# One branch to a whole copy of an expert, in place of a branch in each of its steps

## The chip, the cores and the metric

The kernel runs on one core of a Trainium2 chip. Times are device microseconds of one execution; less is better. The kernel before takes 1640.35 us, the median of 3 runs.

## The reference

The program is a two-layer encoder on 512 tokens of 1024 features. Layer 0 has a neighbourhood attention and a dense SwiGLU; layer 1 has a latent attention and a mixture of eight experts, of which each token takes two. The change touches the experts alone. There the reference runs every expert on all tokens and weighs the results; the weight is zero where a token has not chosen the expert:

```python
probs = softmax(hf @ w_router)
vals, idx = lax.top_k(probs, 2)
wts = vals / jnp.sum(vals, axis=-1, keepdims=True)
combine = jnp.sum(one_hot(idx, 8) * wts[..., None], axis=1)
y = 0
for e in range(8):
    gate, up = split(hf @ w_gu[e], 2)          # 1024 x 3584
    y = y + combine[:, e:e+1] * ((silu(gate) * up) @ w_down[e])   # 1792 x 1024
```

## The kernel before

The experts are called e0 to e7 here, as the code counts them; the words of the change, "two to seven", are e1 to e6. The kernel gathers for each expert only the rows that chose it. How many these are is known when the program runs, not before. The first 128 rows are the first block, done for every expert; rows 129 to 256 are the second block. A second block of at most 64 rows is done in the form "few" (its rows packed beside each other, `few_rows`, 8 or 16 matmuls where the whole form has 24), a larger one in the form "many", and an expert with 128 rows or fewer has none. In the traced execution e1 is few, e2 and e7 are many, and e0, e3, e4, e5 and e6 have no second block, as the lines show that run in them.

An expert has 11 steps. Steps 0 to 6 multiply the rows by gate and up weights (24 matmuls of 128 x 512 a block), make `act`, and transpose it in the next step into `A` (`turn`, `store_turn`). Steps 7 to 10 multiply `A` by the down weights. Each weight arrives by DMA (queued by SP), is cast to a rounded high part `hi` by ACT, and VectorE subtracts to get the low part `lo`; three matmuls (hi x hi, hi x lo, lo x hi) make one product in nearly full precision. `emit_to` issues the loads and casts of a later step beside the matmuls of this one.

The order is written out by hand: on each engine the instructions stand in the order of the code, and the loop over `steps` is unrolled. What depends on the number of rows stands in branches. `second_block(n, many, few)` is a branch on the register `n` (L1483) and within it one between many and few (L1487), on every engine. Two of them stand in every step. One runs the matmuls of the second block. The other, `flush()`, runs what the step before owed to the second block (the list `pend`): its `act`, its transposes' copies, or its output. The copy that is taken of a branch and the one that isn't must leave the semaphores with the same counts; in a path that skips work, an engine therefore waits until its own earlier work is done and then adds the skipped ticks, in one semaphore instruction. `count(e)` (L1479) loads the number of rows of an expert to a register of each engine; it stands in step 1 of the expert ahead (step 3 for e0). The rows of the next expert are gathered there and transposed in steps 7 and 8 (`rows0`), those of its second block in step 9 (`second_rows`).

Of the kernel before, what the change touches and what calls it, by code (L numbers as in the profile page):

```python
# [9 lines left out]
F32 = mybir.dt.float32  # L10
# [46 lines left out]

class Kernel:
    def __init__(self, ctx, tc, d, dbg=None):
        self.ctx, self.tc, self.nc, self.d = ctx, tc, tc.nc, d  # L60
        self.dbg = dbg
        pool = lambda name, bufs, **kw: ctx.enter_context(tc.tile_pool(name=name, bufs=bufs, **kw))
        self.consts = pool("consts", 1)
        self.big = pool("big", 3)
        self.rawp = pool("raw", N_RAW)
        self.splitp = pool("split", N_SPLIT)
        self.dram = pool("dram", 1, space=DRAM)
        self.Y = self.dram.tile([(NE - 1) * CAP, D], F32, name="Y")
        self.jobs = []
        self.done = {}  # L70
        self.emitted = 0
        self.loaded = {}
        self.ada_acc = None
        self.ada_rows = []
        self.extra = None
        self.raw_slots, self.raw_no = [], -1
        self.piece = self.pool_every = 0

    def add_slots(self, pool, n, big, raw_pool, n_raw):
# [3 lines left out]
        self.slots = ["split"] * N_SPLIT + ["extra"] * n + ["big"] * big  # L83
        self.raw_slots = [raw_pool] * n_raw + [0, 1] + [self.rawp] * N_RAW
# [46 lines left out]
    def raw_tile(self, shape):  # L131
# [5 lines left out]
        t = self.big_raw[:, pool] if pool in (0, 1) else pool.tile([P, 2048], F32, name="raw", tag="raw")  # L137
# [5 lines left out]
    def split_tiles(self, shape, pool=None):  # L143
        n = int(np.prod(shape[1:]))
        kind = "split"
        if pool is None and self.extra is not None:
            self.turn_no += 1
            kind = self.slots[self.turn_no % len(self.slots)]
        if kind == "big":
            both = [self.big_split[:, i, 0:n] for i in range(2)]  # L150
        else:
            pool = pool or (self.extra if kind == "extra" else self.splitp)
            both = [pool.tile([P, 2048], F32R, name=w, tag=w)[:, 0:n] for w in ("hi", "lo")]
# [935 lines left out]
    def router(self, small, hp, ps_a, ps_b, ps_c, cst):  # L1089
# [64 lines left out]
        def rest(R, C, T, idx0, ps_y):  # L1154
# [41 lines left out]
            ps = ps_y.tile([P, S], F32, name="y", tag="y")  # L1196
# [12 lines left out]
            ps = ps_y.tile([P, S], F32, name="y", tag="y")  # L1209
# [19 lines left out]
    def moe_phase(self, xT, oH, oL):  # L1229
        nc, tc, d = self.nc, self.tc, self.d  # L1230
        with ExitStack() as es:
# [64 lines left out]
            self.add_slots(split, N_EXTRA, N_BIG, turns.enter_context(tc.tile_pool(name="moe_raw", bufs=N_RAWX)), N_RAWX)  # L1296
            A = st.tile([P, 14, 512], F32R, name="a")
# [9 lines left out]

            def rows_tile():
                return w1.tile([P, D], F32, name="xb")
# [15 lines left out]
            def rows0(he, t, h, b=0, ps=None):  # L1325
                if ps is None:
                    ps = ps_t.tile([P, S], F32, name="tp", tag="tp")
# [42 lines left out]
            def out_rows(e, n, b, ps):  # L1370
                yo = w2.tile([P, S], F32, name="yo")
# [3 lines left out]

            def act_tile():
                return w2.tile([P, 256], F32, name="act0")
# [23 lines left out]
            def few_out(e, n, ps):  # L1401
                gs = w2.tile([P, S], F32, name="yo")[0:FEW]
# [5 lines left out]
            def overflow():  # L1408

                iota, tokid = cst[:, 0:128], cst[:, 128:132]  # L1410
                with tc.tile_pool(name="over", bufs=1, side="right") as op:
# [4 lines left out]
                    ps = ps_t.tile([P, S], F32, name="tp", tag="tp")  # L1416
# [10 lines left out]
                    with tc.For_i(0, NE, 1) as e:  # L1427
# [10 lines left out]
                        for j in range(7):  # L1438
                            pss = [ps_gu.tile([P, S], F32, name="gu", tag="gu") for _ in range(2)]
# [6 lines left out]
                            for b in range(2):  # L1446
                                a = act_tile()
                                swiglu(a, pss[b])
                                ps = ps_t.tile([P, S], F32, name="tp", tag="tp")
                                turn(a, ps)  # L1450
                                store_turn(A, j, b, ps)
                        for n in range(2):
                            pss = [ps_y.tile([P, S], F32, name="y", tag="y") for _ in range(2)]
# [6 lines left out]
                            for b in range(2):  # L1460
                                t = w2.tile([P, S], F32, name="yo")
                                nc.vector.tensor_scalar_mul(t, pss[b], cur[:, 1, 0, b:b + 1])
                                yo.append(t)
                            for i in range(4):
                                ps = ps_gu.tile([P, S], F32, name="gu", tag="gu")
# [8 lines left out]
                for i in range(4):  # L1474
                    for n in range(3):
                        self.square_sum(x_tok, w2, ssq, n, i)
# [3 lines left out]

            def second_block(n, many, few):

                with tc.If(n > P):  # L1483
# [34 lines left out]
            tail = rest(scratch[:, 0:1024], scratch[:, 1024:1280], w2.tile([P, S], F32, name="yo"), idx0, ps_y)  # L1518
            next(tail)
            for i in range(4):  # L1520
                for h in range(2):
                    ps = ps_gu.tile([P, S], F32, name="gu", tag="gu")
# [8 lines left out]
            rows0(he_next, xb0, 1, ps=ps_y.tile([P, S], F32, name="y", tag="y"))  # L1531
# [10 lines left out]
            def weigh(cols, ps, b=0):  # L1542

                for b, p in enumerate(ps, b):
                    t = w2.tile([P, S], F32, name="yo")[:, cols]
# [4 lines left out]
            for i, (e, s) in enumerate(steps):  # L1550
                emit_to(2 * i + PRE)
                n, g = divmod(s - 7, 2)
                ws = [self.done[k][0:2] for k in step_jobs(i)]
                if s == 0:
                    n_reg, he = n_next, he_next
                    act0 = None
                if s == (3 if e == 0 else 1) and e < last:
                    n_next = count(e + 1)
                    xb0 = rows_tile()
                    gather(xb0, HT, idx, 4 * (e + 1))  # L1560
                    with tc.If(n_next > P):
                        gather(xb1, HT, idx, 4 * (e + 1) + 1)
                owe = lambda *f: pend.append(f)
                if s < 7 or g == 0:
                    second.reverse()
                    ps1 = second[0]
                parts = [ALL] if e < last or s < 9 else HALVES if s == 9 else HALVES[0:1]
                if s < 7:
                    ps = ps_gu.tile([P, S], F32, name="gu", tag="gu")
                    for t in range(2):  # L1570
                        gate_up(ps, he, 0, t, ws[t])
                    flush()
                    pend_reg, pend_few = n_reg, e < last
                    prev, act0 = act0, act_tile()
                    swiglu(act0, ps)
                else:
                    if g == 0:
                        pys = [ps_y.tile([P, S], F32, name="y", tag="y") for _ in parts]
                        py = pys[0]
                    for b, cols in enumerate(parts):  # L1580
                        for t in range(2):
                            down(pys[b], A, 0, 2 * g + t, ws[t], cols)
                    flush()
                    prev = act0 if s == 7 else None
                if prev is not None:
                    ps = ps_t.tile([P, S], F32, name="tp", tag="tp")
                    turn(prev, ps)
                    store_turn(A, s - 1, 0, ps)
                    owe(lambda A=A, j=s - 1: store_turn(A, j, 1, tp1), lambda A=A, j=s - 1: few_store(A, j))
                if s < 7:  # L1590
                    owe(lambda ps=ps1: swiglu(act1, ps), lambda ps=ps1: few_swiglu(ps))

                def many():
                    for t in range(2):
                        if s < 7:
                            gate_up(ps1, he, 1, t, ws[t])
                    if s >= 7:
                        for ps, cols in zip(second, parts):
                            for t in range(2):
                                down(ps, A, 1, 2 * g + t, ws[t], cols)  # L1600
                    if prev is not None:
                        turn(act1, tp1)

                def few():
                    for t in range(2):
                        if s < 7:
                            few_rows(ps1, he, ws[t], 4 * t, 4 * t + 4, KD)
                        else:
                            k0 = 8 * g + 4 * t
                            few_rows(ps1, A, ws[t], k0, min(14, k0 + 4), 14)  # L1610
                    if prev is not None:
                        few_turn()

                if i == 0:
                    second_rows(n_reg, he, True, second[1])
                second_block(n_reg, many, few if e < last else None)
                if s >= 7 and g == 1 and e < last:
                    out_rows(e, n, 0, py)
                    owe(lambda e=e, n=n, ps=ps1: out_rows(e, n, 1, ps), lambda e=e, n=n, ps=ps1: few_out(e, n, ps))
                if e == last:  # L1620
                    if s == 0:
                        turns.close()
                        late = pool("moe_late", 1)
                        self.raw_slots = [self.rawp]
                        gf_row = late.tile([P, D], F32, name="gf_row")
                        fn_row = late.tile([P, D], F32, name="fn_row")
                        x_tok = self.big_raw.rearrange("p a (b c) -> p (a b) c", b=2)
                        nc.scalar.dma_start(gf_row, self.GF.broadcast_to([P, D]))
                        nc.scalar.dma_start(fn_row, d["final_norm"].rearrange("(o n) -> o n", o=1).broadcast_to([P, D]))
                        for t in range(4):  # L1630
# [199 lines left out]
```

## Time and profile before

| | |
|---|---|
| median of 3 runs | 1640.35 us (1640.19 to 1643.37) |
| profiled execution: its time | 1640.96 us |
| its span | 1639.2 us |
| PE (TensorE) busy | 1568.3 us, 96% |
| VectorE busy | 1109.6 us, 68% |
| ACT (ScalarE) busy | 817.1 us, 50% |
| experts e0 to e7, start to end | 927.9 to 1639.2 us of the span |
| e3, e4, e5, e6: from first matmul to that of the next expert | 65.9, 66.2, 66.0, 67.2 us |

An expert without a second block has 14 x 2 + 8 small transposes and 252 large matmuls, one each 0.23 us. PE's matmul instructions are taken up by a sequencer that runs ahead of the array; branches, register loads and semaphore instructions run on that sequencer (PEq and PEldq in the rows), and they are not counted as busy. An idle time in brackets is put down to what came last by the trace before the instruction started.

### The profile page before, as it was taken

Reading aid. Unit: us, or ns where it says so; the run is one execution under the profiler, and the core shown is the slowest. Engines: PE = TensorE matmul, PEld = TensorE weight load, DVE = VectorE, ACT = ScalarE, POOL = GpSimd, SP = SyncE. Lnnn points to the kernel's source line nnn. Section 1 sums busy time; section 2 is a strip of 40 time slices with the busy share of each in tenths; the row PEclk is TensorE's granted clock in tenths of the full one; section 3 lists DMA queues with packets and bytes.
Section 4 is the critical chain, followed back from the end, with each engine's and each line's share of the span. In section 5 each row is a group of like instructions: output and inputs, shape, how many; then the busy total and the mean of one; then the engine's idle time right before and its main releaser. Section 6 shows DMA issues by size and latency. Waiting matters only on the chain. (4 is left out here: it accounts for less than half of the span.)

```text
span 1639.2 us, 23888 instructions
## 1 busy us (share of the span) xinstructions
PE 1568.3 (96%) x8293; PEld 1266.4 (77%) x8293; DVE 1109.6 (68%) x1701; ACT 817.1 (50%) x1382; POOL 295.3 (18%) x250
## 2 busy tenths in 40 slices
PE   6899999999999999999999989999999999999996
PEld 4677779888888888877778677778887777777886
DVE  5787856765655644688865668656437888887765
ACT  3465544422222123577764656645446677775442
POOL 0332310002000000000001443112123323233310
PEclk9999999999999999999999989999999999999998
DMA  9545533467544643201021599667468999997851
GB/s 354 191 140 167 176 114 103 144 213 254 198 159 151 229 154 113 78 26 52 27 81 54 198 367 353 240 206 260 158 205 298 330 351 358 342 371 263 260 197 53
DMA packets 241212, 327.43 MB, mean 200 GB/s; under 512 B 9586, under 2 KB 191570, under 8 KB 240404
## 3 DMA queue, kind: packets, MB, share of 16 engines
q1 hardware_dynamic: 231072, 296.19, 54.2%
q0 software_dynamic: 5232, 18.09, 3.1%
q10 hardware_dynamic: 4740, 11.02, 1.9%
q8 instruction: 92, 1.51, 0.4%
q14 instruction: 76, 0.62, 0.1%
HBM read 308.75 MB, written 16.52 MB: 198 GB/s over the span
## 5 line engine op out<-in xcount | busy, mean ns | idle before, releaser
L193 DVE TENSOR_TENSOR lo<-raw,hi 128x1024 fp32r<-128x1024 f32 (+1 forms) x280 | 371.6, 1359 | 89.2 <-ACT hi L190 80.4
L190 ACT CAST hi<-raw 128x1024 fp32r<-128x1024 f32 (+1 forms) x313 | 312.0, 1045 | 225.5 <-PE mm L291 147.4
L291 PE MATMUL mm<-hL,hi 128*128 128x512 f32 x480 | 190.8, 398 | 0.0
L290 PE MATMUL mm<-hH,hi 128*128 128x512 f32 x480 | 190.3, 396 | 0.1
L292 PE MATMUL mm<-hH,lo 128*128 128x512 f32 x480 | 190.1, 396 | 0.0
L1344 PE MATMUL gu<-hi,he 128*128 128x512 f32 x360 | 144.5, 401 | 9.8 <-ACT act L1354 4.0
L1346 PE MATMUL gu<-hi,he 128*128 128x512 f32 x360 | 141.3, 392 | 0.0
L1345 PE MATMUL gu<-lo,he 128*128 128x512 f32 x360 | 140.8, 391 | 0.0
L193 POOL TENSOR_TENSOR lo<-raw,hi 128x1024 fp32r<-128x1024 f32 x37 | 96.9, 2619 | 227.6 <-ACT hi L190 163.0
L220 DVE SCALAR_TENSOR_TENSOR ada_acc<-raw,c_act,ada_acc 128x1024 f32<-128x1024 f32 x70 | 90.6, 1294 | 36.8 <-DMA raw<-in_w_ada_dram 36.0
L290 PEld LDWEIGHTS mm<-hH,hi 128*128 128x128 f32 x480 | 90.6, 189 | 20.8 <-ACT hi L190 0.5
L291 PEld LDWEIGHTS mm<-hL,hi 128*128 128x128 f32 x480 | 90.4, 188 | 20.0 <-issue 1.0
L292 PEld LDWEIGHTS mm<-hH,lo 128*128 128x128 f32 x480 | 90.4, 188 | 19.2 <-issue 0.2
L1344 PEld LDWEIGHTS gu<-hi,he 128*128 128x128 f32 x360 | 67.6, 188 | 30.7 <-issue 7.8
L1354 ACT ACTIVATE act<-gu 128x256 f32<-128x256 f32 x56 | 21.5, 384 | 138.2 <-PE gu L1346 137.8
L193 DVE TENSOR_TENSOR lo<-raws,hi 128x1024 fp32r<-128x1024 f32 x50 | 70.9, 1451 | 14.2 <-ACT hi L190 12.5
L1346 PEld LDWEIGHTS gu<-hi,he 128*128 128x128 f32 x360 | 67.6, 188 | 15.6 <-DVE he L204 0.4
L1344 PE MATMUL y<-hi,a 128*128 128x512 f32 (+1 forms) x200 | 77.5, 387 | 2.2 <-PEq L1483 1.7
L1345 PEld LDWEIGHTS gu<-lo,he 128*128 128x128 f32 x360 | 67.7, 188 | 13.3
L371 DVE SCALAR_TENSOR_TENSOR xT<-mm,mod,xT 128x512 f32<-128x512 f32 (+1 forms) x52 | 32.5, 626 | 66.3 <-PE mm L292 66.2
L321 POOL TENSOR_TENSOR rs<-rs 128x2 f32<-128x2 f32 (+1 forms) x8 | 2.7, 336 | 407.4 <-DVE rs L319 407.4
L1346 PE MATMUL y<-hi,a 128*128 128x512 f32 (+1 forms) x200 | 75.4, 377 | 0.0
(405 smaller groups left out, 3702.4 us busy)
## 6 DMA issues: line engine op xcount, KB each, us to landing
raw<-in_moe_w_gu_dram SPq DMA_DIRECT2D x176, 512.0 KB
raw<-in_w_ada_dram SPq DMA_DIRECT2D x48, 1024.0 KB
raw<-in_moe_w_down_dram SPq DMA_DIRECT2D x37, 1024.0 KB
raws<-in_moe_w_gu_dram SPq DMA_DIRECT2D x48, 512.0 KB
raw<-in_ffn_w_gu_dram SPq DMA_DIRECT2D x22, 1024.0 KB
raw<-in_na_w_qkv_dram SPq DMA_DIRECT2D x12, 1024.0 KB
raws<-in_moe_w_down_dram SPq DMA_DIRECT2D x11, 1024.0 KB
raw<-in_ffn_w_down_dram SPq DMA_DIRECT2D x8, 1024.0 KB
```

The lines of the kernel that those rows point to most:

```text
L190: nc.scalar.copy(hi[:, c], raw[:, c])
L193: eng.tensor_tensor(lo[:, c], raw[:, c], hi[:, c].bitcast(F32), op=OP.subtract)
L220: nc.vector.scalar_tensor_tensor(acc, raw[:, i], c, acc, op0=OP.mult, op1=OP.add)
L290: nc.tensor.matmul(ps, ah, bh, start=first, stop=False)
L291: nc.tensor.matmul(ps, ah, bl, start=False, stop=False)
L292: nc.tensor.matmul(ps, al, bh, start=False, stop=last)
L321: g.tensor_tensor(w, y, y, op=OP.mult)
L371: self.nc.vector.scalar_tensor_tensor(x, ps[:, tok], self.mcol(layer, which, m), x, op0=OP.mult, op1=OP.add)
L1344: nc.tensor.matmul(ps, xh, wh, start=first, stop=False)
L1345: nc.tensor.matmul(ps, xh, wl, start=False, stop=False)
L1346: nc.tensor.matmul(ps, xl, wh, start=False, stop=last)
L1354: nc.scalar.activation(a, ps[:, 0:256], AF.Silu)
```

## The change

The loop over 88 steps becomes a function `one_expert`. It is called once for e0 and once for e7, with the branches in each step as before. For e1 to e6 it is called three times each, with `way[0]` set to many, few or none, and `second_block` then runs the one form directly, with no branch. The three copies stand one behind the other in every engine's program, in the order many, few, none, under one nested branch at the start of the expert. The tiles that rotated in pools are held in rings, so that the copies use the same buffers and end in the same state.

Four things move with that. `count(e + 1)` stands at the start of expert e, ahead of the branch. What the last step owes (`flush`) stands at the end of its copy. The transposes of the second block's rows stand in step 0 of their own expert, and no longer in step 9 of the one before, save for e7, whose branch stays in step 9 of e6. POOL loads the count once more for its gather (`n_pool`).

```diff
@@ -1473,13 +1499,19 @@
+            way = [None]
+
             def second_block(n, many, few):
 
+                if way[0] is not None:
+                    if way[0]:
+                        (many if way[0] == "many" else few)()
+                    return
                 with tc.If(n > P):
                     if few is None:
                         many()
@@ -1542,142 +1574,191 @@
...
+            def one_expert(this):
...
+                    if s == (3 if e == 0 else 1) and e < last:
+                        if e == 0:
+                            n_next = count(1)
+                        xb0 = rows_tile()
+                        gather(xb0, HT, idx, 4 * (e + 1))
+                        n_pool = nc.values_load(cnt[0:1, e + 1:e + 2], engines=[ET.Pool], min_val=0, max_val=S)
+                        with tc.If(n_pool > P):
+                            gather(xb1, HT, idx, 4 * (e + 1) + 1)
...
+                    if s == 0 and way[0]:
+                        (rows1 if way[0] == "many" else rows1_few)(he, second[1])
...
+                        if s == 9 and e + 1 == last:
+                            with tc.If(n_next > P):
+                                rows1(he, second[1])
...
+            def branch(e, kind):
+
+                way[0] = kind
+                one_expert(e)
+                flush()
+                way[0] = None
+                return self.emitted, self.turn_no % len(self.slots), self.raw_no % len(self.raw_slots), self.piece, [id(t) for t in second], [r.no for r in rings]
+
+            n_reg = n_next
+            one_expert(0)
+            for e in range(1, NE):
+                flush()
+                n_reg = n_next
                 if e == last:
...
+                    one_expert(e)
+                    break
+                n_next = count(e + 1)
+                begin = state()
+                with tc.If(n_reg > P) as two:
+                    with tc.If(n_reg > P + FEW) as wide:
+                        ends = [branch(e, "many")]
+                    with wide.Else():
+                        restore(begin)
+                        ends.append(branch(e, "few"))
+                with two.Else():
+                    restore(begin)
+                    ends.append(branch(e, ""))
+                assert ends[0] == ends[1] == ends[2]
             flush()
             order.close()
```

The first place is PE's program within an expert, between the last matmul of a step and the first of the next (`tp` takes the transposes of `act`; `second_...` is the buffer of the second block). Before:

```order
L1346 MATMUL gu<-hi,he 128x512
L1483 COMPARE_AND_BRANCH
L1487 COMPARE_AND_BRANCH
L1487 UNCONDITIONAL_BRANCH x2
L1483 UNCONDITIONAL_BRANCH
L1359 MATMUL tp<-ident,act_15820 128x128 x2
L1483 COMPARE_AND_BRANCH
L1487 COMPARE_AND_BRANCH
L1344 MATMUL second_8382<-hi,he 128x512
```

The same place in a none copy of the change:

```order
L1373 MATMUL gu<-hi,he 128x512
L1374 MATMUL gu<-lo,he 128x512
L1375 MATMUL gu<-hi,he 128x512
L1388 MATMUL tp<-ident,act_8577 128x128 x2
L1373 MATMUL gu<-hi,he 128x512
L1374 MATMUL gu<-lo,he 128x512
```

Both branches are gone, and the transposes stand between two groups of matmuls with nothing else.

The second place is PE's program from the end of e1 to the start of e2. Before, the last rows are those of e1's second block:

```order
L1383 MATMUL second_8381<-hi,a 128x512
L1383 MATMUL second_8381<-lo,a 128x512
L1487 UNCONDITIONAL_BRANCH
L1483 UNCONDITIONAL_BRANCH
L1344 MATMUL gu<-hilo,he 128x512
L1345 MATMUL gu<-hilo,he 128x512
```

In the change it is the end of e1's none copy, the last of the three, and the start of e2's many copy (`xb_8391` holds the rows of the second block):

```order
L1374 MATMUL y<-lo,a 128x512
L1375 MATMUL y<-hi,a 128x512
L1752 UNCONDITIONAL_BRANCH
L1505 TENSOR_LOAD cnt
L1752 COMPARE_AND_BRANCH
L1753 COMPARE_AND_BRANCH
L1343 MATMUL tp_8383<-ident,xb_8391 128x128 x4
L1343 MATMUL second_8381<-ident,xb_8391 128x128 x4
L1373 MATMUL gu<-hilo,he 128x512
```

The load of the count, two branches and the transposes of the second block have come between the experts.

The third place is VectorE's program at the end of e1's few form (`yo` is the output of the second block). Before, the addition stands in the branch of step 0 of e2:

```order
L193 TENSOR_TENSOR lo<-raw,hi 128x1024 x2
L193 TENSOR_TENSOR lo<-raws,hi 128x1024 x2
L1483 COMPARE_AND_BRANCH
L1487 COMPARE_AND_BRANCH
L1487 UNCONDITIONAL_BRANCH
L1404 TENSOR_TENSOR yo<-second_8381,yo 64x512
L1487 UNCONDITIONAL_BRANCH
```

In the change it is the last row of the copy, ahead of the jump over the none copy:

```order
L1430 TENSOR_TENSOR yo<-second_8382,yo 64x512
L218 TENSOR_TENSOR hilo<-raw,hilo 128x1024 x2
L218 TENSOR_TENSOR lo<-raw,hi 128x1024 x3
L218 TENSOR_TENSOR lo<-raws,hi 128x1024 x2
L1430 TENSOR_TENSOR yo<-second_8381,yo 64x512
L1753 UNCONDITIONAL_BRANCH
```

What reads and frees the buffer `second_8381` has moved ahead of the next expert's first rows.

## Rows read from the trace of the kernel before

**Rows 1.** The page: each engine's busy time, share of the span and instructions.
```profile
PE 1568.3 (96%) x8293; PEld 1266.4 (77%) x8293; DVE 1109.6 (68%) x1701; ACT 817.1 (50%) x1382; POOL 295.3 (18%) x250
```

**Rows 2.** Windows of e2, e4, e5, part of e6; last columns clock, DMA share, GB/s.
```profile
1111.00:1232.00 121.00, 120.85 (x545) 98.40 (x544) 60.04 (x69) 55.69 (x80) 22.69 (x14) 1.00 0.64 211
1297.36:1363.60 66.24, 62.84 (x274) 49.33 (x275) 55.72 (x52) 46.89 (x61) 21.68 (x11) 1.00 1.04 350
1363.60:1429.58 65.98, 62.75 (x274) 49.12 (x275) 55.61 (x52) 46.66 (x61) 21.42 (x11) 1.00 1.04 349
...
1450.00:1470.00 20.00, 19.55 (x87) 15.43 (x86) 16.88 (x18) 14.89 (x21) 5.71 (x2) 1.00 1.06 377
```

**Rows 3.** Branch line L1483, e3 to e6: nanoseconds min/median/max, first and last start.
```profile
L1483 PEldq COMPARE_BRANCH  x87: 70/208/458, 1232.9 to 1490.6; - x87
...
L1483 PEldq EVENT_SEMAPHORE  x46: 51/51/51, 1237.1 to 1490.5; - x46
```

**Rows 4.** The waits of PE in e3 to e6.
```profile
PE gu L1344 <- ACT act L1354: 5.4, 8, 1.1
```

**Rows 5.** PE in order of time, e5: start us, us, line, operation, [idle before].
```profile
1368.63 0.39 PE L1345 MATMUL gu<-lo,he 128*128 128x512 f32 x1
1368.86 0.39 PE L1346 MATMUL gu<-hi,he 128*128 128x512 f32 x1
...
1376.60 0.47 PE L1344 MATMUL gu<-hilo,he 128*128 128x512 f32 x1 [0.35 <-ACT act L1354]
...
1388.23 0.38 PE L1359 MATMUL tp<-ident,act 128*128 128x128 f32 x2
1388.76 0.47 PE L1344 MATMUL gu<-hi,he 128*128 128x512 f32 x1
...
1423.97 0.39 PE L1346 MATMUL y<-hilo,a 128*128 128x512 f32 x1
1424.92 0.47 PE L1344 MATMUL y<-hi,a 128*128 128x512 f32 x1 [0.57 <-PEq L1483]
...
1428.89 0.39 PE L1346 MATMUL y<-hi,a 128*128 128x512 f32 x1
1429.58 0.47 PE L1344 MATMUL gu<-hi,he 128*128 128x512 f32 x1 [0.30 <-PEq L1483]
```

**Rows 6.** Line L1479, the load of a count.
```profile
L1479 PEldq TENSOR_LOAD <-cnt x8: 306/314/498, 918.6 to 1435.6; - x8
```

**Rows 7.** Line L1695, the branch over the overflow part.
```profile
L1695 PEldq COMPARE_BRANCH  x1: 3552/3552/3552, 1626.8 to 1626.8; - x1
L1695 DVEq COMPARE_BRANCH  x1: 63/63/63, 1627.5 to 1627.5; - x1
```

**Rows 8.** One branch of PE in e2, and PE in order of time behind it.
```profile
L1487 PEldq COMPARE_BRANCH  x1: 169/169/169, 1129.7 to 1129.7; - x1
...
1133.33 0.38 PE L1359 MATMUL tp<-ident,act 128*128 128x128 f32 x2
1133.47 0.48 PE L1344 MATMUL gu<-hi,he 128*128 128x512 f32 x1
```

**Rows 9.** A wait of PE, and windows behind it and at the end.
```profile
76.12 0.35 PE L687 MATMUL s<-kT,qH 128*128 128x256 f32 x1 [4.14 <-DVE kT L204]
...
77.10:80.40 3.30, 3.30 (x12) 2.83 (x11) 3.27 (x11) 3.27 (x9) 1.40 (x2) 0.50 0.73 282
...
1626.70:1630.40 3.70, 0.37 (x4) 0.17 (x2) 2.55 (x10) 1.37 (x7) 0.00 (x0) 0.97 0.03 9
```

**Rows 10.** VectorE and ACT by line near the end of e1.
```profile
L193 DVE TENSOR_TENSOR lo<-raws,hi 128x1024 fp32r<-128x1024 f32 x2 | 2.4, 1223 | 0.3 <-ACT hi L190 0.3
...
L1404 DVE TENSOR_TENSOR yo<-second,yo 64x512 f32<-64x512 f32 x1 | 0.7, 673 | 0.0
...
L1403 ACT COPY yo<-second 64x512 f32<-64x512 f32 x1 | 0.6, 587 | 0.0
```

**Rows 11.** What ACT's casts of weights waited for, e4 and e5.
```profile
  DMA raw<-in_moe_w_gu_dram: 1.2, 2
```

More of the change, by code (lines that the diff above doesn't have):

```diff
@@ L76, in __init__ @@
         self.raw_slots, self.raw_no = [], -1
+        self.held = {}
         self.piece = self.pool_every = 0
@@ L144, in split_tiles @@
         n = int(np.prod(shape[1:]))
-        kind = "split"
-        if pool is None and self.extra is not None:
+        make = lambda pool: [pool.tile([P, 2048], F32R, name=w, tag=w) for w in ("hi", "lo")]
+        if pool is not None or self.extra is None:
+            both = make(pool or self.splitp)
+        else:
             self.turn_no += 1
[L148 to L153, printed above, removed]
+            slot = self.slots[self.turn_no % len(self.slots)]
+            if slot[0] == "big":
+                both = [self.big_split[:, i] for i in range(2)]
+            else:
+                if slot not in self.held:
+                    self.held[slot] = make(self.extra if slot[0] == "extra" else self.splitp)
+                both = self.held[slot]
+        both = [t[:, 0:n] for t in both]
         return [v.rearrange("p (a b) -> p a b", a=shape[1]) for v in both]
@@ L1549, in moe_phase @@
             last = NE - 1
[L1550 to L1580, printed above, removed]
-                        for t in range(2):
[L1582 to L1598, printed above, removed]
@@ L1599, in many @@
                             for t in range(2):
-                                down(ps, A, 1, 2 * g + t, ws[t], cols)
+                                down(pys[b], A, 0, 2 * g + t, ws[t], cols)
+                        flush()
+                        prev = act0 if s == 7 else None
                     if prev is not None:
[L1602 to L1612, printed above, removed]
@@ new lines, in many, with few @@
+                    def many():
+                        for t in range(2):
+                            if s < 7:
+                                gate_up(ps1, he, 1, t, ws[t])
+                        if s >= 7:
+                            for ps, cols in zip(second, parts):
+                                for t in range(2):
+                                    down(ps, A, 1, 2 * g + t, ws[t], cols)
+                        if prev is not None:
+                            turn(act1, tp1)
+                    def few():
+                        for t in range(2):
+                            if s < 7:
+                                few_rows(ps1, he, ws[t], 4 * t, 4 * t + 4, KD)
+                            else:
+                                k0 = 8 * g + 4 * t
+                                few_rows(ps1, A, ws[t], k0, min(14, k0 + 4), 14)
+                        if prev is not None:
+                            few_turn()
@@ new lines, in one_expert @@
+                    if s >= 7 and e < last:
+                        if s in (7, 8):
+                            rows0(he, xb0, s - 7, ps=new_gu())
+                        if s == 9 and e + 1 == last:
+                            with tc.If(n_next > P):
+                                rows1(he, second[1])
+                    emit_to(2 * i + POST)
+                    if i == 0:
+                        for t in range(4):
+                            nc.scalar.dma_start(XT[t * P:(t + 1) * P], x_tok[:, t])
@@ new lines, in one_expert, with state, restore @@
+                    if 1 <= i < 3:
+                        next(tail)
+                    if i == 2:
+                        idx, dest, wm, tab = (self.rt[n] for n in ("idx", "dest", "wm", "tab"))
+            def state():
+                return (dict(self.done), self.emitted, dict(self.loaded), self.turn_no, self.raw_no, self.piece, list(second), pend_reg, pend_few,
+                        [r.no for r in rings], xb0)
+            def restore(z):
+                nonlocal pend_reg, pend_few, xb0
+                done, self.emitted, loaded, self.turn_no, self.raw_no, self.piece, order2, pend_reg, pend_few, nos, xb0 = z
+                self.done, self.loaded = dict(done), dict(loaded)
+                second[:] = order2
+                for r, no in zip(rings, nos):
+                    r.no = no
```

228 lines of the change are left out of this document (133 added, 95 removed).

## The prediction

> **What bounds the kernel now.** The page comes first: TensorE (PE) is busy for 96% of the span and the chain that ended last runs through it [rows 1]. So the time is PE's matmuls plus the gaps between them, and the question is which gaps the change closes and which it opens. The windows by expert come next [rows 2]. An expert with a second block of rows (e2) keeps PE at over 99% (of the busy times that follow the length, PE's is the first); one without (e3 to e6; four of them, of some 66 us each) leaves PE unoccupied for about 3.2 us, and its DMA moves 349 to 350 GB/s, against 377 GB/s in the densest stretch of 20 us. The clock is granted in full (1.00) in all of them.
>
> The rows of the branch line tell where the gaps come from [rows 3]. Between 1226 and 1491 us PE's sequencer runs 87 outer branches, and 46 semaphore instructions in the paths that skip; these wait for PE's own earlier matmuls and then add the skipped ticks. The largest entry in the waits of PE [rows 4] is ACT's `act`, eight times; but in the order of time [rows 5] the wait of 0.97 us "for act" stands between two matmul groups that share nothing with `act`, at the step in which the count is loaded. I read it as the same drain plus the load (0.31 us, [rows 6]) plus the branches.
>
> What a gap costs beyond the pitch of 0.23 us (1368.63 to 1368.86), in e5 [rows 5]: 1370.22 - 1368.86 - 0.23 = 1.13 us where the count is loaded; from the transposes at 1388.23 to the next matmul 0.53 us, where an expert that takes its branch needs 0.14 us (1133.33 to 1133.47, [rows 8]), so 0.39 us, at seven places; at 1376.60 the marked wait is 0.35 where the others show none, some 0.59 in all; 1424.92 - 1423.97 - 0.23 = 0.72; and 0.46 at the start of the next expert (1429.58).
>
> **What it removes.** In the copies of e3 to e6 no step branches, so none drains: 1.13 + 7 x 0.39 + 0.59 + 0.72 = 5.2 us for each expert, 20.7 us for four. From below it is the 3.2 us of each in which PE wasn't busy, 12.9 us. I take the upper one, since the order shows nothing left between the matmuls. The start of e7 needs no count and no branch ahead of it: 0.5 us. In e1 and e2 I take nothing, since the branches there run ahead of PE (99% busy in e2, [rows 2]). Together 21.2 us.
>
> **What it adds: long jumps.** A copy without a second block stands last; PE's program skips some 2,030 instructions to reach it (1,100 to the few copy, 1,480 from the end of a many copy, 550 from the end of a few copy; a matmul counts as two). The near branches take 0.07 to 0.46 us on PE [rows 3]. The one far jump of before, over the unused overflow part (1,180 instructions), took 3.55 us on PE, and 0.06 on VectorE, where it skips 180 [rows 7]. I take 3.55 for each PE jump of this length; from below it is 0.2 us, and from above nothing in the trace shows it. [...]
>
> How much of it PE feels depends on the sequencer's lead. The branch that starts at 1129.7 stands just ahead of the matmul of 1133.47: it ran 3.6 us before PE needed it [rows 8]. That is the cover where nothing drains.
> - e0 to e1: e0 keeps its branches, and its last skip drains PE. The load, a near and a far branch are then bare: the 1.13 us of the step that loads the count, 0.2 and 3.55, less the 0.46 of before: +4.4 us.
> - e1 to e2: the few copy's last output is now added on VectorE at the end of the copy, behind its casts, and the next copy begins with transposes into the same buffers. ACT copies it (0.59 us), VectorE has a subtraction in front (1.22) and adds (0.67) [rows 10]: 2.5 us, and 1.3 with nothing in front, 4.6 behind two long ones. The jump hides behind this. I take +2.6.
> - e2 to e3: two far jumps and the load, 3.55 + 0.31 + 3.55 + 0.2 = 7.6 us, less 3.6 of cover: +4.0.
> - e3 to e4, e4 to e5, e5 to e6: one far jump each, 0.31 + 3.55 + 0.2 - 3.6 = 0.5 us and a restart of 0.16, where 0.46 stood: +0.6 for all three. Without cover it is 3.6 us more at each.
>
> **The clock.** [...] I take +4.1.
>
> **DMA.** An expert moves 349 GB/s x 65.98 us = 23.0 MB. Without its gaps the period is 65.98 - 5.2 - 0.46 + 0.7 = 61.0 us, which asks for 377 GB/s: just what the densest 20 us reached [rows 2]. The casts of e4's and e5's weights waited only 1.2 us for DMA [rows 11], so there is some lead to use up; I charge 0.5 us for each of e4 to e6, +1.5, with 0 and 15 us (349 GB/s again) as bounds.
>
> The moved transposes of the second block (from step 9 to step 0) and the extra count load of POOL are the same work on engines or at places with room: the PE instructions are the same in number, and POOL is busy for about a third of an expert (21.4 of 66 us, [rows 2]). ACT's and VectorE's own jumps are of 240 to 280 instructions; at 0.06 us each they cost nothing, and at a PE-like price they would be covered by the idle time that both have in an expert (19 and 10 us, [rows 2]).
>
> **Sum:** -21.2 + 4.4 + 2.6 + 4.0 + 0.6 + 4.1 + 1.5 = -4.0 us. The profiled execution took 1640.96 us, so 1637.0; the median of the runs lies 0.6 lower, so 1636.4 us. A change of 0.2%, 3.3 us, is about the least that a measurement of this kernel can tell: 1637.07 and 1643.63 are the lines.
>
> **The rivals.**
> - *Dearer jumps (slower).* The 3.55 us was taken while DMA moved 9 GB/s [rows 9]; the new jumps come while it moves 211 to 350 GB/s [rows 2], and a fetch would queue with the weights. Six jumps are bare or have their cover used up (one, two, and three), so each added microsecond costs 6 us: 2 us more gives 1648.4. It is slower by over 0.2% from 1.2 us more. The same comes if the sequencer's lead isn't there at the copies' ends. For it: the load; against: the near branches of the loaded stretch aren't longer than 0.46 us, though these may fetch nothing.
> - *DMA becomes the bound.* If e4 to e6 can't go beyond 355 GB/s, a period is 64.9 us, 3.9 above the forecast's: 1636.4 + 11.7 - 1.5 = 1646.6; at 365 GB/s 1641. For it: these experts already stand at 350 with a DMA share of 1.04; against: 377 was reached, and casts hardly waited.
> [...]
> - *The clock doesn't fall.* 4.1 us less: 1632.3. For it: with one core's matmuls dense on both sides, three gaps of 2 to 4 us may pass; against: [rows 9].
>
> **How the numbers follow.** The forecast's own case has 0.36 (1633 to 1641), dearer jumps 0.20 (1640 to 1650), DMA 0.14 (1641 to 1650), cheap jumps 0.17 (1624 to 1629), the clock 0.13 (1630 to 1634). The likeliest gives 1636.4. Faster: half of the first, nearly all of the last two, 0.47. Slower: two thirds of the second and third and a little of the first, 0.26. Within 0.2%: 0.27. The range from 1626 to 1648 leaves out some 0.08 below and 0.10 above.
>
> **What would show it.** In the profile of after: e3 to e6 at 61 us each with no PE gap inside a copy; PE's compare branches at the copies at 3.5 us; PE gaps of about 5, 2.6 and 4 us at the starts of e1, e2 and e3, and half clock for some 3 us behind them; 0.5 us gaps at e4, e5, e6; DMA at 370 GB/s or more in e4 to e6. Wrong is the removed part if e3 to e6 stay above 63 us with no wait for DMA; the jumps if they take under 1 or over 4.7 us; the DMA term if ACT's casts wait for weights by several microseconds an expert.

## The result, and the profile after

The change is slower: 1660.0 us median of 4 runs (1658.21 to 1662.64), against 1640.27 us; the ratio is 1.0117, 95% interval 1.0099 to 1.0135. The profiled execution's span is 1658.1 us, 18.9 more than before.

The waits of PE, with their releasers, are other ones than before [rows 4]; four of those in the experts (the total in us, how often, the longest):

```profile
PE gu L1373 <- ACT hi L215: 12.3, 3, 4.1
...
PE tp L1369 <- issue: 6.6, 1, 6.6
PE gu L1373 <- issue: 6.4, 1, 6.4
...
PE tp L1343 <- issue: 3.3, 1, 3.3
```

That is six waits, one at the start of each of e1 to e6 (e0 has two of its own for POOL, 3.7 us together; the others up to e6 are of at most 0.7 us). Inside the copies none is left of those in [rows 5]. The three of 4.1 us are put down to ACT's cast, but what they stand beside is in the rows of PE's branch line from 1230 to 1500 us (ns, min/median/max):

```profile
L1752 PEldq COMPARE_BRANCH  x4: 6487/6604/6620, 1245.3 to 1445.3; - x4
```

and, of the same program, in those of the inner branch line at the end of e2's copy:

```profile
L1753 PEldq COMPARE_BRANCH  x1: 3515/3515/3515, 1241.3 to 1241.3; - x1
```

The one far jump of before took 3.55 us [rows 7]; those ahead of e3 to e6 take 6.5 to 6.6 us, and ahead of e3 the one of 3.5 us comes first. PE in order of time at the start of e4:

```profile
1314.40 0.39 PE L1375 MATMUL y<-hi,a 128*128 128x512 f32 x1
1318.94 0.76 PE L1373 MATMUL gu<-hi,he 128*128 128x512 f32 x1 [4.15 <-ACT hi L215]
1319.50 0.63 PE L1374 MATMUL gu<-lo,he 128*128 128x512 f32 x1
1319.93 0.63 PE L1375 MATMUL gu<-hi,he 128*128 128x512 f32 x1
...
1321.63 0.54 PE L1373 MATMUL gu<-hi,he 128*128 128x512 f32 x1
1322.01 0.40 PE L1374 MATMUL gu<-lo,he 128*128 128x512 f32 x1
1322.24 0.39 PE L1375 MATMUL gu<-hi,he 128*128 128x512 f32 x1
```

The branch ran from 1312.15 to 1318.77 us, and the first matmul came 0.17 us later. Then the pitch is 0.43 us instead of 0.23: seven matmuls take 3.07 us (1318.94 to 1322.01) instead of 1.59. The windows of the jump, of the slow matmuls, of the jump at 1241, and of the experts e4 and e6 (length, busy us of PE, PEld, DVE, ACT, POOL, then clock, DMA share, GB/s):

```profile
1312.15:1318.77 6.62, 2.64 (x12) 1.87 (x10) 6.62 (x5) 4.45 (x6) 3.96 (x2) 0.98 1.10 351
1319.00:1321.60 2.60, 2.60 (x6) 2.06 (x7) 2.60 (x3) 0.20 (x1) 0.00 (x0) 0.50 1.07 365
1241.35:1244.87 3.52, 3.52 (x17) 2.94 (x16) 1.74 (x2) 3.30 (x4) 0.55 (x1) 1.00 0.72 218
...
1318.94:1385.02 66.08, 62.04 (x275) 50.36 (x275) 55.68 (x52) 46.47 (x61) 23.14 (x10) 0.96 1.04 350
...
1452.05:1514.77 62.72, 62.72 (x283) 51.34 (x284) 52.11 (x52) 43.11 (x58) 20.12 (x9) 0.98 0.92 316
```

The clock stands at 0.50 behind the gap, from 1319.00 to 1321.60 us. e4 takes what it took before (66.08 against 66.24, [rows 2]): its drains are gone, and the gap at its end with the slow start has taken their place. e6, whose end has no branch, is at 62.7 us. The jump of 3.5 us fell in a stretch with 218 GB/s, those of 6.6 with 324 to 351.

Where the 18.9 us are, by the starts of the experts' first matmuls: to e1 7.1, e1 5.6, e2 7.8, e3 1.1, e4 -0.2, e5 1.1, e6 -4.4, e7 to the end 0.9.

### The profile page after: what moved, and what is told of

It reads as the page before. It is cut to its first block, busy times and chain, and to the rows that moved or that the text cites. A ratio compares the mean times of both kernels' runs of the same rounds, so it can differ in the third digit from the quotient of the medians.

```text
span 1658.1 us, 22724 instructions
## 1 busy us (share of the span) xinstructions
PE 1573.1 (95%) x8293; PEld 1278.3 (77%) x8293; DVE 1111.7 (67%) x1701; ACT 815.0 (49%) x1382; POOL 305.8 (18%) x250
## 5 line engine op out<-in xcount | busy, mean ns | idle before, releaser
L1373 PE MATMUL gu<-hi,he 128*128 128x512 f32 x360 | 148.8, 413 | 20.7 <-ACT hi L215 12.3
L1374 PE MATMUL gu<-lo,he 128*128 128x512 f32 x360 | 144.6, 402 | 0.0
L1375 PE MATMUL gu<-hi,he 128*128 128x512 f32 x360 | 144.4, 401 | 0.0
L218 POOL TENSOR_TENSOR lo<-raw,hi 128x1024 fp32r<-128x1024 f32 x37 | 101.2, 2737 | 228.2 <-ACT hi L215 200.6
L1373 PEld LDWEIGHTS gu<-hi,he 128*128 128x128 f32 x360 | 70.4, 196 | 38.4 <-issue 21.3
L1384 DVE TENSOR_TENSOR act<-act,gu 128x256 f32<-128x256 f32 x56 | 23.4, 417 | 99.6 <-ACT act L1383 98.6
L1375 PEld LDWEIGHTS gu<-hi,he 128*128 128x128 f32 x360 | 69.8, 194 | 16.4 <-DVE he L229 0.4
L1373 PE MATMUL y<-hi,a 128*128 128x512 f32 (+1 forms) x200 | 77.1, 386 | 0.1
```

What stands on the lines that cost most here:

```text
L218: eng.tensor_tensor(lo[:, c], raw[:, c], hi[:, c].bitcast(F32), op=OP.subtract)
L1373: nc.tensor.matmul(ps, xh, wh, start=first, stop=False)
L1374: nc.tensor.matmul(ps, xh, wl, start=False, stop=False)
L1375: nc.tensor.matmul(ps, xl, wh, start=False, stop=last)
L1384: nc.vector.tensor_mul(a, a, ps[:, 256:512])
```

## The experiments

My theory after the result: a far jump of PE waits for the fetch of its target, the fetch waits behind the weight stream, and what PE's queue doesn't cover becomes a gap and costs the clock. The rivals: the distance of the jump sets its price; the load of the count or the ticks at the branch make the gap; and VectorE, not the jump, holds e1 and e2, since the moved transposes wait for it. Each run below stood beside runs of the kernel before, whose median was 1640.6 to 1641.5 us (1640.27 beside the change), so a difference between two runs holds to about 1 us.

**No far jump (own_copy).** The branch stays with everything around it, but only the copy that these inputs take is there; no work is left out that the inputs need.

```diff
+            KINDS = lambda e: {1: ["few"], 2: ["many"]}.get(e, [""])
...
+                kinds = KINDS(e)
+                ends = []
                 with tc.If(n_reg > P) as two:
                     with tc.If(n_reg > P + FEW) as wide:
-                        ends = [branch(e, "many")]
+                        if "many" in kinds:
+                            ends.append(branch(e, "many"))
                     with wide.Else():
+                        if "few" in kinds:
+                            restore(begin)
+                            ends.append(branch(e, "few"))
+                with two.Else():
+                    if "" in kinds:
                         restore(begin)
...
+                        ends.append(branch(e, ""))
```

> The branch ahead of each of e1 to e6 stays, with its load of the count, but only the copy that these inputs take stands behind it (few for e1, many for e2, none for e3 to e6), so that no jump is long. If the far jumps cost the time: the gaps at the starts of e1 and e3 (6.8 and 6.6 us) fall to under 2 and to 0.5 us, those of e4, e5, e6 (4.2 to 4.3 us) to 0.5, and the half clock behind them goes (1.2 to 2.4 us each); the gap at e2 stays at 3 to 4 us, since the addition of yo on VectorE ends it there. In all 27 to 33 us less than the change, about 1629 us. If DMA then binds e4 to e6, these stay at 64 us or more and the time is about 1638. If the gaps come from the load of the count or the ticks at the branch, not from the jump: still 1655 to 1660.

Measured: 1629.42 us, ratio to before 0.9928 (0.9913 to 0.9943), 30.6 less than the change. The windows of e4 and e5, and of a wait at e1:

```profile
1301.48:1362.12 60.64, 60.64 (x275) 49.30 (x274) 59.86 (x52) 46.59 (x60) 23.36 (x11) 1.00 1.08 364
1362.12:1422.53 60.41, 60.41 (x275) 49.29 (x274) 59.75 (x52) 46.59 (x60) 23.19 (x11) 1.00 1.08 364
...
1003.60:1008.90 5.30, 0.12 (x2) 0.03 (x1) 5.10 (x5) 2.77 (x4) 0.00 (x0) 0.62 1.09 359
```

PE is busy without a break in e4 and e5, clock 1.00, with the load of the count (0.3 us) and a near branch (0.2 us) still ahead of each: these run within the lead of PE's sequencer and cost nothing. So the jumps themselves made the gaps at e3 to e6, and DMA was no bound. One part of the expectation failed: I had the gap at e1 fall to under 2 us. PE's waits there and at e2:

```profile
PE second L1369 <- DVEq L1515: 5.2, 1, 5.2
PE second L1343 <- DVE yo L1430: 3.8, 1, 3.8
```

With no jump, e1's transposes wait as long for VectorE, which works on five subtractions of weights in that window (5.10 of 5.30 us) ahead of the ticks that the transposes need. Two causes stood one behind the other in that gap.

**No far jump from e3 on (own_copy_late).** As the change for e1 and e2, with `kinds` of the none copy alone for e3 to e6.

> As the change for e1 and e2, with all three copies; e3 to e6 have only the none copy behind their branch. If the far jumps cost the time: the gaps at the starts of e3 to e6 go (6.6 and three of 4.2 to 4.3 us, with their half clock), some 24 us less than the change, 1634 to 1637 us, and 6 to 8 us more than with all far jumps gone. If the jump isn't the cause: 1655 to 1660.

Measured: 1633.12 us, ratio 0.9955 (0.9939 to 0.9970): 26.9 less than the change and 3.7 more than own_copy, where I had expected 6 to 8. The gaps at e1 and e2 are still there:

```profile
PE tp L1369 <- issue: 7.3, 1, 7.3
PE tp L1343 <- issue: 3.3, 1, 3.3
```

So taking their jumps away (own_copy) gained little: as the rival for e1 and e2 has it.

**The transposes back (own_rows9 and change_rows9).** Both put the second block's transposes back in step 9 of the expert before, one in own_copy, one in the change.

```diff
-                    if s == 0 and way[0]:
-                        (rows1 if way[0] == "many" else rows1_few)(he, second[1])
...
-                        if s == 9 and e + 1 == last:
-                            with tc.If(n_next > P):
-                                rows1(he, second[1])
+                        if s == 9:
+                            kind, way[0] = way[0], None
+                            second_rows(n_next, he, e + 1 < last, second[1])
+                            way[0] = kind
```

> As own_copy (no far jump), and the second block's transposes stand again in step 9 of the expert before, in a branch of their own. If VectorE's queue is what the moved transposes wait for (gaps of 1.9 + 5.3 us at e1, 4.0 at e2 in own_copy): both gaps go to under 2 us, with the half clock at e1, and the copies of e2 to e5 get a drain of 0.5 to 0.8 us each: 6 to 10 us less than own_copy, 1619 to 1624 us. If VectorE is late whatever stands there, the wait goes to the next matmul and the time stays at 1628 to 1632.

> The change with all three copies, only the second block's transposes back in step 9 of the expert before. If the far jump and the wait for VectorE stand one behind the other in the same gap, undoing one of them gives nothing at e1 (still some 6.8 us, now the jump alone) and 0.4 us at e2; the drains at step 9 cost 0.5 to 0.8 us each: 1658 to 1664 us, the same as the change or a little more. If they add up: 6 to 10 us less than the change, about 1651.

Measured: own_rows9 1620.88 us, ratio 0.9875 (0.9860 to 0.9890), 8.5 less than own_copy. Its PE in order of time at e1 and at e2:

```profile
1005.50 0.39 PE L1375 MATMUL y<-hi,a 128*128 128x512 f32 x1
1007.20 0.50 PE L1373 MATMUL gu<-hi,he 128*128 128x512 f32 x1 [1.31 <-ACT yo L1401]
...
1110.99 0.40 PE L1409 MATMUL second<-lo,a 128*128 128x512 f32 x1
1111.23 0.40 PE L1373 MATMUL gu<-hilo,he 128*128 128x512 f32 x1
```

The gap at e1 is 1.3 us and the one at e2 is gone: the moved transposes were what waited for VectorE. change_rows9 took 1667.61 us (1662.37 to 1668.70), ratio 1.0164 (1.0149 to 1.0180). Undoing the move with the jumps in place gains nothing, as expected; the gaps at e1 and e2 are 6.5 and 2.9 us, now of the jumps. But it is 7.6 us slower than the change (6.4 by the kernels before beside them), and I had allowed 4. The profiled execution is the shortest of the four (1662.37 us; the others took 1667.42 and more), so most of this stands in no trace. It shows one place, at the start of e5:

```profile
1377.20 0.40 PE L1375 MATMUL y<-hilo,a 128*128 128x512 f32 x1
1387.04 0.59 PE L1373 MATMUL gu<-hi,he 128*128 128x512 f32 x1 [9.44 <-issue]
```

The branch there ended at 1381.09 us; the 5.9 us behind it hold another fetch packet of PE's (queue q8, instruction), started at 1384.44 (1.14 us long). The jump at e4 of the change has such a second packet too, 3.5 us behind its end, but PE was at work by then; here PE starts 1.5 us after that packet's end. Why a second one came while PE stood, no run shows.

**The price of a jump (jump_probes).** The kernel before, with eight branches whose body is PE work and is never entered.

```diff
+            def probe(n, size):
+                ps = ps_t.tile([P, S], F32, name="tp", tag="tp")
+                with tc.If(n > CAP):
+                    for _ in range(size):
+                        nc.tensor.transpose(ps[:, 0:P], self.ident, self.ident)
...
                 second_block(n_reg, many, few if e < last else None)
+                for size in PROBES.get((e, s), ()):
+                    probe(n_reg, size)
```

> The kernel before, with eight branches added that are never taken into their body and skip PE work only: 140, 276, 550 and 1017 matmuls (twice as many instructions), once each under the weight stream of e4 and e5 (about 350 GB/s) and once each late in e7 (under 200 GB/s, the last two with almost nothing). If the load on DMA sets the price: about 6.5 us for the 550 and 1017 in e4 and e5, and 3.5 to 4 us for the same late in e7, with no difference by distance between them. If the distance sets it: the 1017 takes near twice the time of the 550 in both places, and the two places agree. For the 140 and 276 neither theory of mine is firm: 0.2 us if the target is already on the core, as dear as the others if not.

Measured (one run, 1690.83 us), by the records of these branches and the windows over them:

| instructions skipped | place | DMA, GB/s | branch, us |
|---|---|---|---|
| 2034 | e4 | 383 | 6.31 |
| 1100 | e5 | 382 | 6.26 |
| 552 | e4 | 317 | 4.13 |
| 280 | e5 | 293 | 4.53 |
| 2034 | late in e7 | 5 | 3.57 |
| 552 | late in e7 | 7 | 4.88 |
| 1100 | late in e7 | 7 | 4.69 |
| 280 | e7, step 8 | 41 | 0.35 |

```profile
1326.65:1332.96 6.31, 0.00 (x0) 0.00 (x0) 5.10 (x5) 4.08 (x5) 2.43 (x1) 0.79 1.04 383
...
1641.69:1645.26 3.57, 2.06 (x18) 1.85 (x16) 0.00 (x0) 0.00 (x0) 0.00 (x0) 1.00 0.02 5
```

Under the weight stream (382 and 383 GB/s) the jump over 2034 instructions cost what the one over 1100 cost, and 2.7 us more than late in e7, at 5 GB/s. The distance rival falls. The quiet ones are not all at 3.5 to 4 us: those of 4.69 and 4.88 came with two fetch packets of 1.5 to 2.0 us at once, so that the pair over 552 instructions shows nothing of the load. The two of 4.13 and 4.53 us fell where DMA moved less than in the first and third row, and their packets started 1.7 and 2.0 us after the branch, against 3.8 in those two. The jump over 280 instructions costs 0.35 or 4.53 us; what decides there is open.

**Less queued (change_raw6).** `N_RAWX = 1` in place of 3, that is six raw buffers for weights. In e7 the tokens take two of these buffers over, which may then still hold weights that are needed, so that e7 may be computed with other weights than its own; the jumps read here come earlier.

> The change with six raw weight buffers of 1 MB in place of eight, so that less is queued on DMA when the jump's fetch comes. If the fetch waits behind the queued weights: PE's far branches in e3 to e6 take 4.5 to 5.7 us instead of 6.5 to 6.6, the gaps at e4 to e6 fall from 4.2 to 2 to 3.3 us, and the time is 3 to 8 us less, unless casts now wait for DMA. If the distance or the code itself sets the price: 6.5 us as before.

Measured: 1657.65 us, ratio 1.0100 (1.0084 to 1.0115), and the same branches:

```profile
L1752 PEldq COMPARE_BRANCH  x4: 6569/6590/6647, 1245.4 to 1445.4; - x4
```

A miss. Fewer buffers leave DMA as busy (348 GB/s over the jump at e4) and the jump as dear; those at e1 and e2 are even longer, 6.6 and 7.2 us (5.2 and 6.8 in the change). What makes the run 2 to 4 us shorter than the change is not shown. So either the number of loads that SP has out is not what the fetch waits behind, or two buffers less don't change that number.

**The weight stream cut (change_thin).**

```diff
+            self.thin = key[0] in ("egu", "edn") and 3 <= key[1] <= 6
...
+            if self.thin:
+                self.nc.sync.dma_start(raw[:, 0:1, c0:c0 + src.shape[2]], src[:, 0:1])
+                break
             self.nc.sync.dma_start(raw[:, :, c0:c0 + src.shape[2]], src)
```

> The change with the weight loads of e3 to e6 cut to an eighth (gate and up) and a quarter (down); the casts and matmuls run on what stands in the buffers, so these four experts are computed with weights that are mostly not theirs. All instructions and jumps on PE are the change's. If a jump's fetch waits behind the weight stream: PE's far branches at e4, e5 and e6 take 3.5 to 4 us in place of 6.6, the gaps there fall from 4.2 to 0.5 to 1.2 us and the clock keeps its level, the second jump at e3 takes about 3.5; some 18 to 22 us less than the change, 1638 to 1643 us. If distance, place in the program or the branch itself sets the price: 6.6 us and gaps of 4.2 as before, 1655 to 1660 us.

Measured: 1641.38 us (10 runs), ratio 1.0010 (0.9998 to 1.0022), 18.6 less than the change. The profiled execution is one of the two longest, 1647.35 us. The branches at e4, e5, e6, and a window over the first:

```profile
L1758 PEldq COMPARE_BRANCH  x3: 3500/3569/3720, 1313.1 to 1436.4; - x3
```

```profile
1310.00:1320.00 10.00, 8.75 (x39) 6.92 (x38) 10.00 (x7) 7.83 (x9) 4.36 (x3) 1.00 0.26 83
```

The same jumps of PE take 3.5 to 3.7 us where DMA moves 83 GB/s. The gaps at e4 to e6 are 0.9 to 1.3 us, and the clock is 1.00 in that window. This is the theory's main point shown. PE's waits from e3 to e6:

```profile
PE gu L1379 <- issue: 5.0, 1, 5.0
PE gu L1379 <- ACT yo L1407: 3.2, 3, 1.2
```

One part of the expectation failed: at e3 a gap of 5.0 us stays. The first jump there takes 3.7 us and the second 4.9, not 3.5, at 119 GB/s and with two fetch packets at once (1.2 and 2.5 us). In the change that second jump has two packets as well (1.3 and 2.5 us), so cutting the weight stream takes only 1.6 us off its 6.5. What the 3 us at e4 to e6 are is seen in the DMA rows. In the change, in the first 3.85 us of the jump at e4 no packet of PE's instruction queue q8 runs (the first row is all that stands under the queues); it comes in the next 1.4 us:

```profile
q1 hardware_dynamic: 1362, 1.35, 110.3%
...
q1 hardware_dynamic: 477, 0.47, 103.8%
q8 instruction: 1, 0.02, 4.8%
```

By its record the packet starts 3.99 us after the branch in the change, and 1.21 us after it in change_thin; it takes 1.0 to 1.1 us in both, and the branch ends 1.5 us after its end in both.

**Cheaper branches in each step (late_both and else_turn).** If far jumps are the price, the drains can be fought where they are. late_both leaves the kernel before as it is and moves two things behind queued matmuls: `count(e + 1)` with its gather behind the matmuls of its step, and `second_rows` from step 9 to behind the matmuls of step 10.

```diff
                     for t in range(2):
                         gate_up(ps, he, 0, t, ws[t])
+                    if s == (3 if e == 0 else 1) and e < last:
+                        n_next = count(e + 1)
...
                             down(pys[b], A, 0, 2 * g + t, ws[t], cols)
+                    if s == 10 and e < last:
+                        second_rows(n_next, he_next, e + 1 < last, second[1])
                     flush()
```

> The kernel before with its branches in each step; only the load of the count with the gather (from ahead of a step's matmuls to behind them) and the branch with the second block's transposes (from step 9 to behind the matmuls of step 10) are moved to places where PE has work queued. If the lead of PE's sequencer hides what runs behind queued matmuls: the gap of about 1.1 us at the count and the extra 0.4 us of two skips in a row go in each of five experts without a second block, 4 to 7 us less than before, 1634 to 1637 us. If the drain itself is the whole price: within 1 us of before.

Measured: 1634.67 us, ratio 0.9965 (0.9951 to 0.9978), 6.4 less than the kernel before beside it (1641.06). else_turn adds to it that the transposes of `act` stand in both ways of the second block's branch:

```diff
-            def second_block(n, many, few):
+            def second_block(n, many, few, both=None):
 
-                with tc.If(n > P):
+                with tc.If(n > P) as two:
...
+                    if both is not None:
+                        both()
+                if both is not None:
+                    with two.Else():
+                        both()
```

> late_both with its branches in each step, and the transposes of act moved into both ways of the second block's branch (behind the second block's matmuls in the one, alone in the other), so that the way without a second block has PE work of its own in seven of eleven steps. If the drain comes only where a way has no PE work to carry the ticks: the 0.39 us at seven places in each of five experts go, 10 to 14 us less than late_both, 1621 to 1626 us. If any branch costs PE this, whatever stands in it: no change from late_both, 1633 to 1637.

Measured: 1625.71 us, ratio 0.9904 (0.9891 to 0.9918): 9.0 less than late_both, a little under the 10 to 14 expected, and 15.8 less than the kernel before that ran beside it (1641.47). PE's semaphore instructions of the branch line in e3 to e6, first in late_both, then in else_turn:

```profile
L1483 PEldq EVENT_SEMAPHORE  x47: 51/51/51, 1235.9 to 1492.0; - x47
```

```profile
L1483 PEldq EVENT_SEMAPHORE  x19: 51/51/51, 1233.5 to 1478.8; - x19
```

and PE in else_turn, in order of time, in e4:

```profile
1313.45 0.39 PE L1346 MATMUL gu<-hi,he 128*128 128x512 f32 x1
1313.68 0.38 PE L1359 MATMUL tp<-ident,act 128*128 128x128 f32 x2
1313.82 0.48 PE L1344 MATMUL gu<-hi,he 128*128 128x512 f32 x1
```

From the transposes to the next matmul it is 0.14 us where it was 0.53 [rows 5]; 28 drains are gone (seven in each of four experts) and the branches are all there. It is the fastest kernel here that runs for any number of rows; own_rows9 is 4.8 us faster and runs for these inputs alone.

## Why the prediction was wrong

- **What it removes: right.** 5.2 us of drains for each expert without a second block were forecast. In own_copy e5 takes 60.41 us where it took 65.98: 5.6, of which 0.46 is the gap at its end. No gap is left in the copies of e4 and e5.
- **Long jumps: the step that failed.** "I take 3.55 for each PE jump of this length" was the price of the one far jump in the trace, at 9 GB/s. The jumps that count come at 324 to 368 GB/s and take 5.2 to 6.8 us, save the one at 1241 us (218 GB/s, 3.5 us). The sequencer's lead is why the error weighs so much. It was taken as 3.6 us; in the change it is 2.9 at e4 to e6 (at e4 the load of the count starts at 1311.74 us, and the next matmul would have been due at 1314.63) and 4.1 to 4.2 at e2 and e3. So a jump of 3.5 to 3.7 us is nearly covered, with 0.9 to 1.3 us bare in change_thin, while of 6.6 us with the load of the count some 4.2 stay bare. At e4 to e6 the three gaps are 12.3 us together, where 0.46 each stood before, so this term is 11 us instead of 0.6. The gap at e3 is 6.4 us; I had 4.0.
- **e0 to e1:** forecast 4.4 more; the gap is 6.6 us. The jump took 5.2, but it isn't the only cause: own_copy shows that the moved transposes wait as long for VectorE. I saw such a wait only at e2.
- **e1 to e2:** forecast 2.6. PE stands 3.3 us for the jump and then 0.3 for VectorE; without the jump 3.8 us for VectorE (own_copy). The wait for VectorE was there, with a size within the bounds given (1.3 to 4.6), and it is still the last to end, but by 0.3 us only: at 6.8 us the jump no longer hides behind it.
- **The clock: right in kind, too small.** Forecast 4.1 us for three gaps. No run shows this term: it is two and a half times the 1.65 us that a stretch of 3.3 us at 0.50 [rows 9] loses. In the change each of the six gaps brought such a stretch: seven matmuls at half clock behind the gap at e4 cost 1.5 us, and twelve behind the one at e5 2.5 (5.22 us, 1385.02 to 1390.24, instead of 2.72). By the same reckoning it is 1.9 at e1, 1.7 at e2, 2.5 at e3 and 1.5 at e6, some 11.5 us in all.
- **DMA: no bound.** own_copy moves 364 GB/s with PE at 100%: 22.0 MB in the 60.41 us of e5, where 23.0 MB and 377 GB/s were reckoned. The 1.5 us weren't needed.
- **The sum again,** with the measured sizes: removed 4 x 5.2 + 0.5, that is 21.2 as forecast; added 6.1 (e1, less the 0.5 of before), 3.6 (e2), 6.0 (e3), 11 (e4 to e6), 11.5 (the clock) = 38.2: +17.0 us of the 18.9. Of the rest, 0.8 and 0.9 lie ahead of e0's first matmul and behind e7's. Against the forecast's -4.0 that is 21.0 more: 15.1 in the terms of the jumps (those of e1 and e2 with VectorE's part), 7.4 in the clock, and 1.5 less for DMA.
- **The rivals.** "Dearer jumps" is what came; its condition was 1.2 us more a jump, and it is 3. It stood at 0.20, though "nothing in the trace shows it" was said of the upper bound and the range ended at 1648, which is 2 us more for a jump. By the rival's own 6 us for each added microsecond, 3 us more give 1654.4; the clock, which the rival left as it was, lost 7.4 us more than forecast. With a price from one jump at 9 GB/s and nothing to bound it, the range should have gone beyond 1650.

The fetch of which that rival speaks stands in the traces. Each of the nine far jumps of PE in before and in the change took 3.5 us or more, holds a packet of the queue q8 (instruction; two in the second jump at e3), and ended 1.4 to 1.6 us after the end of its last packet; the near ones took 0.21 us in the median [rows 3]. The size and its dependence on the other DMA traffic come from the runs after the result.

What stays open: what in the weight stream the fetch waits behind, since two raw buffers less didn't shorten it; when a jump over 280 instructions is cheap; when two fetch packets come at once, as at e3; and the second fetch in change_rows9.

## What to carry to other kernels

Price a far jump where it will stand: what it costs in a stretch with little DMA was 3 us too little here, and what counts is what remains beyond the lead of the engine's sequencer. Duplicating code to save small waits in each step bought one long fetch or two for each choice; it was cheaper to give the way that skips some work of its own, so that it needn't drain. And when one gap has two causes behind each other, undoing one shows little, as change_rows9 did: take both away in one kernel.

## What the runs showed of the hardware

- A taken branch of PE to code far away (550 to 2034 instructions) took 3.55 to 3.9 us at 5 to 9 GB/s of DMA (before, late in the change, jump_probes), 3.5 to 3.7 us in change_thin at e4 to e6 (83 GB/s around e4) and 3.5 us at 218 GB/s (the change, 1241 us); three with two fetch packets at once took 4.7 to 4.9 us (two in jump_probes at 7 GB/s, one in change_thin at e3). At 324 to 383 GB/s it took 5.2 to 6.8 us (the change, jump_probes, change_raw6 at e4), and one over 552 instructions took 4.1 us at 317 (jump_probes). In the traces of before and of the change the difference is the time until the fetch packet starts: 1.0 us after the branch in the three at 8 to 218 GB/s, 2.1 to 4.1 us in the six of 5.2 us and more. ACT's and VectorE's branches at the same places, over some 240 to 280 instructions by the prediction's count, took at most 0.06 us.
- Each of the six gaps on PE at the starts of the change's experts (3.3 to 6.6 us) was followed by 7 to 12 matmuls of 128x512 at a pitch of 0.43 us in place of 0.23, with the clock at 0.50. So was the gap of 3.8 us at e2 in own_copy, but not at once: the first four went at full pitch, the next seven at 0.43 us. Behind the gap of 1.3 us at e1 in own_rows9 there were none, and the clock was 1.00 in the 10 us around the gap at e4 in change_thin (0.9 to 1.3 us).
- In own_copy the weight stream went at 364 GB/s over e5, with PE busy in all of its 60.41 us.
